# Half-rotary embedding on one core: loads and stores moved from one DMA queue to two

## The chip, the cores and the metric

The kernel runs on 1 core of one Trainium2 chip. The metric is device time in microseconds (us): 161.47 us before, median of 3 runs (161.44 to 161.71). The data lies in HBM, the main memory; the engines work on SBUF, which has 128 partitions. DMA transfers between the two are issued by the engines' sequencers, each into a queue of its own (SP's, ACT's, POOL's), and carried by 16 DMA engines.

## The reference

`x` is float32 of shape (16, 512, 16, 64): batch, sequence, heads, dim. `cos` and `sin` are (512, 32). Only the first half of the last axis is rotated; the second half is copied.

```
half = 32; x1, x2 = x[..., :32], x[..., 32:]
a, b = x1[..., :16], x1[..., 16:]
c, s = cos[..., :16], sin[..., :16]       # broadcast over batch and heads
out  = concat(a*c - b*s, a*s + b*c, x2)
```

Input and output are 33.55 MB each. There is no matrix product.

## The kernel before

**Tiles.** `x`, flat, is cut into T = 4 tiles of 8.39 MB, numbered 0 to 3. In a tile every partition holds K = 16 sequence positions of one batch element, 16 x 16 x 64 floats: 64 KB in one contiguous run in HBM. So a transfer of a whole tile has 128 runs of 64 KB; half a tile (KC = 8 positions) has 128 runs of 32 KB. SBUF holds `ring`, NS = 3 slots of one tile; tile t lies in slot t % 3, so tile 3 takes slot 0 after tile 0 has been stored.

**Tables.** `cos` and `sin` come by POOL's queue into `stage` (L63, L64). A shuffle (L73) and copies (L80, L83) on VectorE (DVE) make `table`, in which each partition has the cosines and sines of its positions.

**Compute.** `rotate(t, lo, hi)` turns half a tile in place with four DVE instructions: `b_t = x1 * s` (L96, into PSUM), `x1 = x1 * c` (L97), a subtraction (L98) and an addition (L101). Two `rotate` make a tile (`turn`), followed by one `store`. All arithmetic is on DVE, in program order: tile 0 to tile 3.

**Transfers.** `load` (L55) and `store` (L58) both issue from SP, so that all of them stand in one queue, in the order of the program. SP works its list strictly in order; an instruction that waits holds back those after it:

1. load 0, load 1, first half of load 2, with nothing to wait for
2. store 0, when tile 0 is rotated
3. second half of load 2
4. positions 0 to 13 of load 3 (KL = 14), which wait until store 0 has landed, since they overwrite its slot; then positions 14 and 15 of load 3
5. store 1, which by an explicit dependency (L115) also waits until the larger part of load 3 has landed
6. store 2 and store 3, each when its tile is rotated

The first `rotate` of a tile waits for the load that holds its half.

Of the kernel before, what the change touches and what calls it, by code (L numbers as in the profile page):

```python
# [1 line left out]

# [4 lines left out]


@with_exitstack
def kernel(  # L10
    ctx: ExitStack,
    tc: tile.TileContext,
    x: bass.AP,
    cos: bass.AP,
    sin: bass.AP,
    out: bass.AP,
):
    nc = tc.nc
    fp32 = mybir.dt.float32
    P = 128  # L20
    B, S, H, D = x.shape
    Q = D // 4
    HF = D // 2

    K = 16
    T = B * S // (P * K)
    PB = S // K
    REP = P // PB  # L30
    R = H * D
    NS = 3
    KC = K // 2
    KL = 14

    xf = x.rearrange("b s h d -> (b s h d)").rearrange("(t p f) -> t p f", t=T, p=P)
    of = out.rearrange("b s h d -> (b s h d)").rearrange("(t p f) -> t p f", t=T, p=P)
    cosf = cos.rearrange("(p k) j -> p (k j)", k=K)
    sinf = sin.rearrange("(p k) j -> p (k j)", k=K)

    const_pool = ctx.enter_context(tc.tile_pool(name="const", bufs=1))
    b_pool = ctx.enter_context(tc.tile_pool(name="bp", bufs=1, space=bass.MemoryType.PSUM))


    ring = const_pool.tile([P, NS, K, H, D], fp32)
    stage = const_pool.tile([P, 2, K, HF], fp32)
    spun = const_pool.tile([P, 2 * K, Q], fp32)
    packed = const_pool.tile([PB, 2 * K, Q], fp32)
    table = const_pool.tile([P, 2, K, 2, Q], fp32)

    def rows(t, lo, hi):
        return ring[:, t % NS, lo:hi].rearrange("p k h d -> p (k h d)")

    def load(t, lo=0, hi=K):
        return nc.sync.dma_start(out=rows(t, lo, hi), in_=xf[t, :, lo * R : hi * R])  # L55

    def store(t, lo=0, hi=K):
        return nc.sync.dma_start(out=of[t, :, lo * R : hi * R], in_=rows(t, lo, hi))  # L58


    nc.vector.memset(stage[:, :, :, 0:Q], 0.0)  # L61
    spread = stage.rearrange("(j b) t k i -> j b t (k i)", b=REP)
    nc.gpsimd.dma_start(out=spread[:, 0, 0], in_=cosf)  # L63
    nc.gpsimd.dma_start(out=spread[:, 0, 1], in_=sinf)  # L64
    load(0)
    load(1)
    load(2, 0, KC)

    PQ = PB // REP
    nc.vector.stream_shuffle(  # L73
        out=spun[:],
        in_=stage.rearrange("p t k j -> p (t k) j")[:, :, 0:Q],
        mask=[j % PQ * REP for j in range(PB)],
    )
    for q in reversed(range(REP)):
        n = PQ * (q + 1)
        nc.vector.tensor_copy(out=packed[0:n], in_=spun[q * PB : q * PB + n])  # L80

    for r in range(REP):
        nc.vector.tensor_copy(  # L83
            out=table[r * PB : (r + 1) * PB].rearrange("p t k c j -> p (t k) c j"),
            in_=packed.unsqueeze(2).to_broadcast((PB, 2 * K, 2, Q)),
        )
    C = table[:, 0].rearrange("p k c j -> p k (c j)")
    Sn = table[:, 1].rearrange("p k c j -> p k (c j)")

    def rotate(t, lo, hi):  # L90
        x1 = ring[:, t % NS, lo:hi, :, 0:HF]
        c = C[:, lo:hi].unsqueeze(2).to_broadcast((P, hi - lo, H, HF))
        s = Sn[:, lo:hi].unsqueeze(2).to_broadcast((P, hi - lo, H, HF))
        b_full = b_pool.tile([P, KC, H, HF], fp32, name="b_t")
        b_t = b_full[:, 0 : hi - lo]
        nc.vector.tensor_mul(out=b_t, in0=x1, in1=s)  # L96
        nc.vector.tensor_mul(out=x1, in0=x1, in1=c)  # L97
        nc.vector.tensor_sub(  # L98
            out=x1[:, :, :, 0:Q], in0=x1[:, :, :, 0:Q], in1=b_t[:, :, :, Q:HF]
        )  # L100
        nc.vector.tensor_add(  # L101
            out=x1[:, :, :, Q:HF], in0=x1[:, :, :, Q:HF], in1=b_t[:, :, :, 0:Q]
        )

    def turn(t):
        rotate(t, 0, KC)
        rotate(t, KC, K)
        return store(t)

    turn(0)  # L110
    load(2, KC, K)
    near = load(3, 0, KL)
    load(3, KL, K)

    tc.add_manual_dep(  # L115
        turn(1).ins,
        near.ins.name,
        mybir.DependencyInfo(mybir.DependencyClass.Sync, mybir.DependencyReason.DATA),
        reason="the store follows the loads at the DMA engines",
    )  # L120
    turn(2)
    turn(3)


# [1 line left out]
_INS = ['x', 'cos', 'sin']  # L126
_OUTS = [((16, 512, 16, 64), 'float32')]


# [23 lines left out]
```

## Time and profile before

| what | value |
|---|---|
| median of 3 runs | 161.47 us |
| the profiled execution, its own time | 162.1 us |
| its span, first to last instruction | 160.3 us |
| DVE busy | 112.4 us (70%), 43 instructions |
| packets of SP's queue, share of 16 DMA engines' span | 97.6% |
| mean DMA rate over the span | 419 GB/s |

The span is the time from the first to the last instruction of the profiled execution; some time lies around it. Engine times are sums of instructions. A DMA engine moves a transfer in packets; the share of a queue is the time that its packets took on all 16 engines. A wait is listed as the instruction that waited, an arrow, and what released it. "SPq" is SP's sequencer, which issues transfers and waits for them. "To landing" is the time from the issue of a transfer to its completion. `L58` is line 58 of the kernel.

### The profile page before, as it was taken

The numbers are of one execution on the slowest core, as the hardware profiler recorded it, in microseconds if no ns is written. First come the engines' busy times: TensorE is split into PE (matmuls) and PEld (weight loads), VectorE is DVE, ScalarE is ACT, GpSimd is POOL, SyncE is SP. The second block draws the span as 40 slices with busy tenths as digits, with TensorE's granted clock in tenths as the row PEclk, the third lists the DMA queues.
The fourth block names the chain that finished last, engine by engine and source line by source line (L and its number), as shares of the span: only waits on it lengthen the run. The fifth ranks groups of instructions, "written<-read, shape, count | busy, mean of one in ns | idle before, by whom it ended". The sixth has DMA issues, their size and how long they took to land.

```text
span 160.3 us, 113 instructions
## 1 busy us (share of the span) xinstructions
DVE 112.4 (70%) x43; POOL 1.4 (1%) x6
## 2 busy tenths in 40 slices
DVE  1000959999999999999999999999999950000000
POOL 3000000000000000000000000000000000000000
DMA  7969969699699996999999995996996996996990
GB/s 262 540 262 540 491 294 523 278 507 491 294 392 441 474 523 262 523 392 392 499 482 458 458 444 253 546 523 262 523 523 262 523 507 278 523 507 278 523 507 16
DMA packets 1504, 67.24 MB, mean 419 GB/s; under 512 B 192, under 2 KB 192, under 8 KB 224
## 3 DMA queue, kind: packets, MB, share of 16 engines
q1 hardware_dynamic: 1440, 67.11, 97.6%
q0 software_dynamic: 64, 0.13, 0.2%
HBM read 33.69 MB, written 33.55 MB: 419 GB/s over the span
## 4 chain that ended last, share of the span: by engine, by line
DVE 59%; DMA 14%; issue 7%; DVEq 1%
DVE b_t L96 22%; DVE ring L97 22%; DMA ring<-in_x_dram 14%; DVE ring L101 10%; DVE ring L98 4%; DVEq L148 1%; DVEq L96 0%
## 5 line engine op out<-in xcount | busy, mean ns | idle before, releaser
L96 DVE TENSOR_TENSOR b_t<-ring,table 128x4096 f32<-128x4096 f32 x8 | 35.5, 4432 | 2.1 <-DMA ring<-in_x_dram 1.9
L97 DVE TENSOR_TENSOR ring<-ring,table 128x4096 f32<-128x4096 f32 x8 | 35.4, 4424 | 0.3
L98 DVE TENSOR_TENSOR ring<-ring,b_t 128x2048 f32<-128x2048 f32 x8 | 18.3, 2287 | 0.3
L101 DVE TENSOR_TENSOR ring<-ring,b_t 128x2048 f32<-128x2048 f32 x8 | 18.2, 2280 | 0.0
L73 DVE LOAD_MASK_SELECT spun<-stage x1 | 0.0, 14 | 14.4 <-DMA stage<-in_sin_dram 14.4
L83 DVE COPY table<-packed 32x1024 f32<-32x1024 f32 x4 | 2.7, 684 | 0.1
L80 DVE COPY packed<-spun 32x512 f32<-32x512 f32 (+3 forms) x4 | 1.7, 416 | 0.1
L61 DVE MEMSET stage<- 128x512 f32 x1 | 0.5, 485 | 0.9 <-PEq L137 0.9
L73 DVE STREAM_SHUFFLE spun<-stage 128x512 f32<-128x512 f32 x1 | 0.7, 723 | 0.0
L63 POOL DMA_DIRECT2D stage<-in_cos_dram x1 | 0.6, 649 | 1.3 <-DVE stage L61 1.3
L64 POOL DMA_DIRECT2D stage<-in_sin_dram x1 | 0.5, 532 | 0.0
L137 POOL MEMSET const-float32-0.0<- 128x1 f32 x1 | 0.1, 93 | 0.2 <-issue 0.2
L137 POOL MEMSET const-bfloat16-1.0<- 128x1 bf16 x1 | 0.1, 95 | 0.0
L137 POOL MEMSET const-uint8-127<- 128x1 uint8 x1 | 0.1, 93 | 0.0
L137 POOL MEMSET const-float32-1.0<- 128x1 f32 x1 | 0.1, 92 | 0.0
## 6 DMA issues: line engine op xcount, KB each, us to landing
ring<-in_x_dram SPq DMA_DIRECT2D x2, 4096.0 KB, 41.4
ring<-in_x_dram SPq DMA_DIRECT2D x1, 7168.0 KB, 26.4
ring<-in_x_dram SPq DMA_DIRECT2D x1, 1024.0 KB, 28.5
stage<-in_cos_dram POOLq DMA_DIRECT2D x1, 64.0 KB, 9.0
stage<-in_sin_dram POOLq DMA_DIRECT2D x1, 64.0 KB, 13.4
out_dram<-ring SPq DMA_DIRECT2D x4, 25.6
ring<-in_x_dram SPq DMA_DIRECT2D x2, 32.0
```

The source lines that it names most:

```text
L61: nc.vector.memset(stage[:, :, :, 0:Q], 0.0)
L63: nc.gpsimd.dma_start(out=spread[:, 0, 0], in_=cosf)
L64: nc.gpsimd.dma_start(out=spread[:, 0, 1], in_=sinf)
L73: nc.vector.stream_shuffle(out=spun[:], in_=stage.rearrange("p t k j -> p (t k) j")[:, :, 0:Q], mask=[j % PQ * REP for j in range(PB)],)
L80: nc.vector.tensor_copy(out=packed[0:n], in_=spun[q * PB : q * PB + n])
L83: nc.vector.tensor_copy(out=table[r * PB : (r + 1) * PB].rearrange("p t k c j -> p (t k) c j"), in_=packed.unsqueeze(2).to_broadcast((PB, ...
L96: nc.vector.tensor_mul(out=b_t, in0=x1, in1=s)
L97: nc.vector.tensor_mul(out=x1, in0=x1, in1=c)
L98: nc.vector.tensor_sub(out=x1[:, :, :, 0:Q], in0=x1[:, :, :, 0:Q], in1=b_t[:, :, :, Q:HF])
L101: nc.vector.tensor_add(out=x1[:, :, :, Q:HF], in0=x1[:, :, :, Q:HF], in1=b_t[:, :, :, 0:Q])
L137: nc = _bacc.Bacc("TRN2", target_bir_lowering=False, num_devices=1)
L148: with _tile.TileContext(nc) as tc:
```

## The change

`load` stays on SP's queue, `store` goes to ACT's queue, which held no transfer before. Load 2 is issued whole (64 KB runs). Load 3 is issued as two halves of 8 positions (32 KB runs) in place of 14 and 2 positions. Store 1 is issued as two halves (32 KB runs), each after the `rotate` of its half. The explicit dependency of store 1 on load 3 goes. What each transfer waits for is otherwise the same: a store for the `rotate` of what it stores, load 3 for the landing of store 0.

```diff
-    KL = 14
...
     def load(t, lo=0, hi=K):
-        return nc.sync.dma_start(out=rows(t, lo, hi), in_=xf[t, :, lo * R : hi * R])
+        nc.sync.dma_start(out=rows(t, lo, hi), in_=xf[t, :, lo * R : hi * R])

     def store(t, lo=0, hi=K):
-        return nc.sync.dma_start(out=of[t, :, lo * R : hi * R], in_=rows(t, lo, hi))
+        nc.scalar.dma_start(out=of[t, :, lo * R : hi * R], in_=rows(t, lo, hi))
...
     load(0)
     load(1)
-    load(2, 0, KC)
+    load(2)
...
-    def turn(t):
+
+    rotate(0, 0, KC)
+    rotate(0, KC, K)
+    store(0)
+    load(3, 0, KC)
+    load(3, KC, K)
+    for lo, hi in ((0, KC), (KC, K)):
+        rotate(1, lo, hi)
+        store(1, lo, hi)
+    for t in range(2, T):
         rotate(t, 0, KC)
         rotate(t, KC, K)
-        return store(t)
+        store(t)
-
-    turn(0)
-    load(2, KC, K)
-    near = load(3, 0, KL)
-    load(3, KL, K)
-
-    tc.add_manual_dep(
-        turn(1).ins,
-        near.ins.name,
-        mybir.DependencyInfo(mybir.DependencyClass.Sync, mybir.DependencyReason.DATA),
-        reason="the store follows the loads at the DMA engines",
-    )
-    turn(2)
-    turn(3)
```

In the changed kernel the four lines of `rotate` are L95, L96, L97 and L100, `load` is L54 and `store` L57.

## The prediction, made before the changed kernel ran

> **What bounds the kernel now.** I read the head of the page first, then its DMA queues, then the waits of SP's queue, then short windows of the DMA view. The page:
>
> ```profile
> span 160.3 us, 113 instructions
> DVE 112.4 (70%) x43; POOL 1.4 (1%) x6
> ...
> q1 hardware_dynamic: 1440, 67.11, 97.6%
> q0 software_dynamic: 64, 0.13, 0.2%
> ...
> L96 DVE TENSOR_TENSOR b_t<-ring,table 128x4096 f32<-128x4096 f32 x8 | 35.5, 4432 | 2.1 <-DMA ring<-in_x_dram 1.9
> ```
>
> The DMA queue is the bound: its packets fill 97.6% of 16 engines' span. 10 transfers x 128 runs are 1280 packets, and the 160 left are 16 completion writes for each transfer, so one packet is one run of a partition. The packet records give 2.418 us for a 64 KB run and 1.213 us for a 32 KB run. An engine moves 67.11 MB / 16 = 64 runs of 64 KB: 64 x 2.418 = 154.8 us. It starts at 1.7 to 2.6 us and its last run ends at about 158.6, so only some 2 us of it are not bare transfer. The chain of waits names DVE for 59% of the span, but DVE ends at 130.6 us and the last store only queues from there. SP's waits show it:
>
> ```profile
> SPq L58 <- DVE ring L101: 57.7, 3, 26.9
> SPq L58 <- DMA ring<-in_x_dram: 46.5, 2, 25.6
> SPq L148 <- DMA out_dram<-ring: 28.3, 1, 28.3
> SPq L55 <- DMA out_dram<-ring: 21.7, 1, 21.7
> ```
>
> Line by line: stores wait for DVE; the store of tile 1 waits for most of load 3; after its last issue SP waits 28.3 us; and load 3 waits 21.7 us for store 0, whose ring slot it takes. All this waiting costs nothing, because the engines always have runs queued. Landings by issue time plus time to landing: load 0 at 0.74 + 22.2 = 23.0, load 1 43.0, store 0 at 49.9 + 22.5 = 72.4, the larger part of load 3 98.9, the rest 101.4, store 1 120.8, store 2 140.0, store 3 at 130.6 + 28.7 = 159.3. DVE runs without a gap from 23.05; one `rotate` takes 13.45 us (4.43 + 4.42 + 2.29 + 2.28 and the gaps; 36.50 - 23.05).
>
> One view says how two queues share an engine: the DMA view from 7 to 13 us, where the cosine and sine tables (POOL's queue) meet load 0 (SP's):
>
> ```profile
> DMA packets 96, 3.28 MB, mean 546 GB/s; under 512 B 16, under 2 KB 16, under 8 KB 48
> ...
> q1 hardware_dynamic: 48, 3.15, 120.9%
> q0 software_dynamic: 48, 0.13, 5.5%
> ```
>
> 48 packets against 48: one of each in turn, though one is 64 KB and the other 4 KB or a 4-byte completion. The records of one engine: table run at 7.298, 64 KB run of x at 7.453, and only at 9.868 the table's completion write. So a completion also waits behind the other queue's run, here 2.4 us. Round trip 9.868 - 7.298 = 2.570 against 0.159 + 2.418 = 2.577: the switch itself is free.
>
> **What the Trainium skill says.** "DMA: Bandwidth & Descriptors", section "Queues, rings and completion order": each DMA engine goes round its queues packet by packet; the 48 to 48 agrees. "Issuing engines are not separate DMA queues": SP's and ACT's DMAs run on the same 16 engines and interleave, so no bandwidth is to be won; no run here has shown ACT's queue yet. "Where 436 GB/s comes from": a ceiling of 435 GB/s; 64 KB in 2.418 us on 16 engines is 433.6, so the rate has no room. "Latency and other measured facts": copies with loads and stores on the sync and scalar queues reach 214 GB/s each way, 428 together; the trace before, one direction at a time, makes 67.11 MB in 156.5 us = 429. Mixing should be about free, by that.
>
> **The change, part by part.** Bytes, runs (1280) and completions (160) stay; DVE's 41 instructions stay in order. SP keeps 5 loads, ACT gets 5 stores of about 0.34 us issue each on an otherwise empty engine: nothing, hidden by runs already queued. Before, the explicit dependency and SP's order gave load 3 the engines alone; now order comes from turns. Walk one engine:
>
> Up to 49.94 nothing differs but that load 2 is whole. Load 1's data ends near 42.6, so load 2 has 4 of its 8 runs done at 52.3. Store 0 is issued at 49.94; an issue took 1.0 to 1.9 us to reach the engines (load 0: issued 0.74, first packets 1.74 to 2.61), so it joins at 52.3. Four runs of each alternate: 8 x 2.418, to 71.6; load 2's completion waits one run more, to 74.5. Needed at 76.83 (start of `rotate` of tile 2): cover 2.3 us, cost nothing. The four left of store 0 run to 81.3, landing 81.7, against 72.4 before. So load 3 is issued 9.4 us later; the first half of store 1, ready since 63.4, fills the engines meanwhile.
>
> Load 3 reaches the engines near 83.3, after two runs of store 1. From 83.7 32 KB runs alternate (2.43 us a pair). The first half of load 3 ends at 83.7 + 8 x 2.43 - 1.2 = 101.9 and, its completion behind a run of store 1, lands at 103.5: just at 103.72, when DVE comes to tile 3; a stall of up to 1 us here goes into the next one. Store 1 ends at about 117.7 with two 32 KB runs of load 3 left; store 2, issued at 103.7, follows it with 64 KB runs. Two short runs, one or two runs of 2.418 between them, and the completion behind such a run: the second half lands at 122.9 (one long run met) to 125.4 (two). The 16 engines have different phases and the last one counts, so I take 125.0. DVE, free at 117.17, now stalls 8 us. The last `rotate` ends at 125.0 + 0.1 + 13.45 = 138.5 instead of 130.6.
>
> Store 2's last run still ends near 139.6 (landing 140.0): the engines did the same work without a hole. Store 3 at 138.5 must reach them by then. Load 0 is the measured case of a tile put on idle engines: 22.2 us from issue to landing, some 0.3 of it the tables' runs. Hidden if issued by 159.3 - 22.0 = 137.3. At 138.5 it lands at 160.5: +1.2 us; since some engines will still be busy when it comes, I take +1.1. Both ends: issue at 136.4 costs 0, at 138.9 1.6, and a stall of the first half cannot add. The other terms: start 0, tail 0, the split of load 3 and store 1 into halves (two runs of 1.213 against one of 2.418, 16 times on an engine) 16 x 0.008 = 0.13, against 8 x 0.007 for the 2.116 and 0.309 us pieces of load 3 and 8 x 0.008 for the halves of load 2, which go: 0. Below nothing: all that is not bare transfer is 2 us, of which 0.6 is the first packet (3.2 us against 2.418) that stays, so a gain over 1 us is excluded.
>
> Sum: span 160.3 + 1.1 = 161.4; this execution took 162.1 with 1.8 around the span, 163.2 then. The median of the runs is 161.47, 0.6 under the profiled one, so 161.47 + 1.1 = 162.6.
>
> **Rivals.** *The cover holds* (not slower): only one long run comes between the last short ones, the second half lands by 123.7, store 3 is issued by 137.3 and the engines never starve: 161.5. The profile is for it in that the 9.4 us of cover (130.6 to 140.0) exceeds the stall of the best phase; against it, 16 phases must all be good. *Mixing costs*: loads and stores at once slow the runs. No hole shows at the switch from load to store at 52.07, but there is no stretch of alternation before. About 44 turns of an engine; 0.03 us each adds 1.3 us of work and makes load 3 later too: 164 to 166. *Stores take two turns for one*: store 1 would end near 110 with load 3 half done, store 2 would go before it, and load 3 end near 139: the last `rotate` 152.5, the end near 175. The 48 to 48 speaks against it. *Order kept anyway*: if SP's loads always went first, load 3 would end near 103 as before and the time stay at 161.5; this goes with the first rival.
>
> **How the numbers follow.** Store 3 late by 0.4 to 2.2 us: 0.50, 161.9 to 163.7. Cover holds: 0.25, 161.2 to 161.8. Mixing costs: 0.17, to 166. Two turns for one: 0.03. A gain of up to 1 us from something not seen: 0.05. The range 161.3 to 165.2 leaves out most of the gain, the tail of mixing and the two-for-one case. Faster by over 0.2% 0.06, within it 0.24, slower 0.70; 0.2% (0.3 us) is about what the measurement can tell.
>
> **What would show it.** Two hardware queues of 720 packets each; store 0 landing near 81.7; DVE waiting about 8 us at L95 for the last load; store 3 issued at 136 to 139; a thin slice of DMA near 140. Right mechanism and wrong phase: the wait is 6 us or less and no thin slice. Mixing shows as runs over 2.418 us, or as a larger share of 16 engines than 97.6% x 160.3 us = 156.5 us. A landing of load 3 past 128 would say that the turns are not one for one.

## The result: 165.61 us against 161.58, and the profile after

The changed kernel takes 165.61 us (median of 4 runs, lowest 165.52), the kernel before 161.58 beside it: a ratio of 1.0248, 95% interval 1.0229 to 1.0266. That is 4.0 us more, where 1.1 was forecast. One of the four executions, the one profiled first, took 168.06 us, because in two of its 16 engines load 3 met one long run more; the lines below are of a second profiled execution, 165.76 us, and are held against a second one of the kernel before, 161.53 us with a span of 159.8.

The page of the changed kernel:

```profile
span 163.6 us, 113 instructions
...
DMA  7959979988999899979899999999988996659955
...
q1 hardware_dynamic: 720, 33.55, 48.6%
q10 hardware_dynamic: 720, 33.55, 47.4%
...
L95 DVE TENSOR_TENSOR b_t<-ring,table 128x4096 f32<-128x4096 f32 x8 | 35.5, 4433 | 13.3 <-DMA ring<-in_x_dram 13.1
```

There are two hardware queues of 720 packets now: q1 is SP's, q10 ACT's. DVE sat idle for 13.3 us ahead of the first instruction of a `rotate`, against 2.1 before. The DMA digits (6, 6 and 5 from 135 to 147 us) are only a hint, since the kernel before has sixes in its row too; the windows below decide.

The timeline says when DVE waited. The columns are start, duration, engine and line, and in brackets the idle time ahead. The start of the last `rotate` in the kernel before, and then three starts in the changed kernel, the second and third of them those of tile 3:

```profile
117.17 4.43 DVE L96 TENSOR_TENSOR b_t<-ring,table 128x4096 f32<-128x4096 f32 x1
```

```profile
90.31 4.43 DVE L95 TENSOR_TENSOR b_t<-ring,table 128x4096 f32<-128x4096 f32 x1
105.38 4.43 DVE L95 TENSOR_TENSOR b_t<-ring,table 128x4096 f32<-128x4096 f32 x1 [1.66 <-DMA ring<-in_x_dram]
128.35 4.43 DVE L95 TENSOR_TENSOR b_t<-ring,table 128x4096 f32<-128x4096 f32 x1 [9.55 <-DMA ring<-in_x_dram]
```

The halves of load 3 land at 105.3 and 128.25 us, and DVE stands still for both. The last `rotate` therefore ends at 141.8 instead of 130.6. The chain of what released what shows the path to it, from store 0 through load 3 to DVE (start, duration, what):

```profile
49.97 32.33 DMA out_dram<-ring
...
82.76 45.49 DMA ring<-in_x_dram
...
128.35 4.45 DVE b_t L95
```

Meanwhile the DMA engines run dry; stretches of the DMA share (columns: stretch, length, DVE, POOL, clock, DMA share, GB/s):

```profile
120.00:139.00 19.00, 10.58 (x3) 0.00 (x0) 1.00 1.01 436
139.50:142.60 3.10, 2.26 (x2) 0.00 (x0) 1.00 0.00 0
```

Every DMA engine stands idle for 2.7 to 3.6 us, from the end of its last run of store 2 (139.2 to 140.0) until store 3 starts (142.6 to 142.8). This is the hole that the experiments below are about. By landings: store 2 lands at 140.33 against 139.45 in the kernel before, 0.88 later; store 3 (162.53 against 158.72) follows it by 22.20 us instead of 19.27, 2.93 more. That makes the 3.81 us between the spans 163.58 and 159.77. The remaining 0.4 lies around the span: 165.76 - 163.58 = 2.18 us against 161.53 - 159.77 = 1.76.

So three sums are to be explained: 2.9 us at the hole, 0.9 us ahead of it, 0.4 us around the span.

### The profile page after: what moved, and what is told of

It is laid out like the page before. It is cut to its first block, busy times and chain, and to the rows that moved or that the text cites. A ratio compares the mean times of both kernels' runs of the same rounds, so it can differ in the third digit from the quotient of the medians.

```text
span 165.9 us, 113 instructions
## 1 busy us (share of the span) xinstructions
DVE 112.3 (68%) x43; POOL 1.4 (1%) x6
## 4 chain that ended last, share of the span: by engine, by line
DMA 62%; DVE 22%; issue 2%; DVEq 1%; SPq 0%
DMA ring<-in_x_dram 42%; DMA out_dram<-ring 20%; DVE b_t L95 8%; DVE ring L96 8%; DVE ring L97 3%; DVE ring L100 3%; DVEq L142 1%; SPq L54 0%; DVEq L95 0%
## 5 line engine op out<-in xcount | busy, mean ns | idle before, releaser
L95 DVE TENSOR_TENSOR b_t<-ring,table 128x4096 f32<-128x4096 f32 x8 | 35.5, 4432 | 15.7 <-DMA ring<-in_x_dram 15.5
L96 DVE TENSOR_TENSOR ring<-ring,table 128x4096 f32<-128x4096 f32 x8 | 35.4, 4424 | 0.3
L97 DVE TENSOR_TENSOR ring<-ring,b_t 128x2048 f32<-128x2048 f32 x8 | 18.3, 2286 | 0.3
L100 DVE TENSOR_TENSOR ring<-ring,b_t 128x2048 f32<-128x2048 f32 x8 | 18.2, 2280 | 0.0
## 6 DMA issues: line engine op xcount, KB each, us to landing
stage<-in_sin_dram POOLq DMA_DIRECT2D x1, 64.0 KB, 13.3
```

Source lines behind the costliest of these rows:

```text
L97: nc.vector.tensor_sub(out=x1[:, :, :, 0:Q], in0=x1[:, :, :, 0:Q], in1=b_t[:, :, :, Q:HF])
L100: nc.vector.tensor_add(out=x1[:, :, :, Q:HF], in0=x1[:, :, :, Q:HF], in1=b_t[:, :, :, 0:Q])
```

## The experiments

### Filling the hole, and making load 3 land sooner

**Store 3 in halves.** Against the changed kernel:

```diff
-    for t in range(2, T):
-        rotate(t, 0, KC)
-        rotate(t, KC, K)
-        store(t)
+    rotate(2, 0, KC)
+    rotate(2, KC, K)
+    store(2)
+    for lo, hi in ((0, KC), (KC, K)):
+        rotate(3, lo, hi)
+        store(3, lo, hi)
```

> The changed kernel, with store 3 issued as two halves, each after its rotate. Theory (the hole): the whole loss is the time in which the engines have nothing to do before store 3, because load 3 lands late. The first half of store 3 is then ready near 120 us, stands behind store 2 and fills the engines from 139 to 149, and the second half comes near 141: time 161.4 to 162.0, no hole, DVE still waiting 8 to 11 us for the last load. Rival (mixing): alternating loads and stores slows the transfers themselves; then the time stays at 163.0 to 165.6 and the engines are busy to the end.

Measured: 163.08 us, ratio to before 1.0103 (1.0084 to 1.0122), 2.5 us under the changed kernel. Its waits, and the DMA share where the hole was:

```profile
DVE b_t L95 <- DMA ring<-in_x_dram: 15.1, 3, 11.2
```

```profile
139.50:142.60 3.10, 3.10 (x2) 0.00 (x0) 1.00 0.98 423
```

DVE waits even longer than in the changed kernel (11.2 us for the last load, against 9.55), and it costs nothing any more: the first half of store 3 covers it. The hole is the large part of the loss. But 1.6 us over the kernel before remain, more than this theory allowed.

**Store 2 in 32 KB runs**, issued at the same moment: `store(2)` becomes `store(2, 0, KC)` and `store(2, KC, K)`, both after its second `rotate`.

> The changed kernel, with store 2 issued as two halves (32 KB runs) at the same moment as before. Theory (turns against long runs): the last three runs of load 3 and its completion each stand behind a 64 KB run of store 2; with 32 KB runs the second half lands 3.5 us sooner, near 124.5 instead of 128, store 3 is issued near 138 and the time is 161.6 to 162.6. Rival (the late start alone): load 3 started too late whatever follows; landing near 127, time 164.5 to 165.6.

Measured: 162.99 us (1.0092, 1.0072 to 1.0111). The second half of load 3 lands at 125.8, DVE waits 6.0 us for it, the hole shrinks to 0.6 us. So the size of the runs in the other queue bears on when load 3 ends. The landing came 1.3 us after the expected one, and the time lies 0.4 us above the expected range; 1.6 us had been left unexplained by the first experiment.

**Store 1 in quarters:**

```diff
-        store(1, lo, hi)
+        store(1, lo, lo + KC // 2)
+        store(1, lo + KC // 2, hi)
```

> The changed kernel, with store 1 issued in four quarters (16 KB runs) at the same moments as its halves. Turns by number: load 3 (32 KB runs) gets two thirds of the engines, its second half lands near 116 and the time is 161.4 to 162.0. For the late start of load 3 (its first run began 3.6 us after the issue, behind four 32 KB runs of store 1): if an engine holds a number of runs ahead, four runs of 16 KB take 2.4 us and load 3 begins 2 to 2.6 us after its issue; if it is a time, it begins 3.4 us or more after it, behind six or seven runs. Rival (shares by bytes): the second half lands past 124, time above 164.

Measured: 162.87 us (1.0088, 1.0066 to 1.0110). With 16 KB runs against 32 KB, load 3 gets two thirds of the engines' time (from 86.5 to 103 us 161 packets of SP's queue against 163 of ACT's, and 66.7% of the time) and lands at 115.6; DVE has no wait at all for it, as its waits show (the 1.8 is load 0's):

```profile
DVE b_t L95 <- DMA ring<-in_x_dram: 1.8, 1, 1.8
```

The turns go by number of runs, not by bytes. The time is again above the expected range. For the late start of load 3, compare who runs right after its issue, at 82.4 us here and 82.3 us with quarters. Changed kernel, DMA view of 82.4 to 86.0 us:

```profile
DMA packets 48, 1.57 MB, mean 437 GB/s; under 512 B 0, under 2 KB 0, under 8 KB 0
...
q10 hardware_dynamic: 47, 1.54, 99.0%
q1 hardware_dynamic: 1, 0.03, 2.1%
```

Quarters, 81.9 to 86.2 us:

```profile
q10 hardware_dynamic: 106, 1.74, 94.1%
q1 hardware_dynamic: 8, 0.26, 14.1%
```

In the first, the 32 KB run of store 1 that is under way at the issue and three more pass on nearly every engine before the first run of load 3 (at 86.0 to 86.8 us); in the second, the 16 KB run under way and mostly six more (at 85.9 to 86.7 us). A fixed number of runs would have been the same four. It is a time, of 3.6 us or more from the issue, or an amount, of some 112 to 128 KB for each engine; these runs can't tell the two apart. Once both run, the turns are even. Changed kernel, 86.5 to 103 us (16 of the 115 are completions, which took a turn each):

```profile
q1 hardware_dynamic: 114, 3.74, 52.4%
q10 hardware_dynamic: 115, 3.24, 45.5%
```

**Store 0 alone.** A first attempt put the second half of load 2 on ACT's queue in the line after `store(0)`:

```diff
-    load(2)
+    load(2, 0, KC)
...
     store(0)
+    nc.scalar.dma_start(out=rows(2, KC, K), in_=xf[2, :, KC * R : K * R])
```

> The changed kernel, with the second half of load 2 issued on ACT's queue behind store 0, so that store 0 has the engines to itself again. Theory (store 0 late): store 0 lands near 73 instead of 82, load 3 is issued 9 us sooner and its second half lands near 117, so that DVE has no wait of more than 1 us after the first load: time 161.4 to 162.0. Rival (the sharing of load 3 and store 1 is the cause, not store 0): the last load lands past 122, time above 163.

Measured: 168.12 us. It doesn't test what it was meant to: the load, which waits for nothing, was placed at the head of ACT's list and ran beside load 0, so that DVE started nearly 10 us late. With an ordering dependency from the load to store 0:

> As l2b_behind_s0 was meant: the second half of load 2 on ACT's queue, issued after store 0 and not ahead of everything. Theory (store 0 late, because it shares the engines with load 2): store 0 lands near 73 to 74, load 3 is issued then, its second half lands near 117 and DVE loses less than 1 us: 162.5 to 163.2, the level of the runs without a hole. Rival (the sharing of load 3 and store 1 is enough): second half past 122, above 164.

Measured: 162.70 us (1.0069, 1.0054 to 1.0084). Store 0 lands at 72.7 instead of 82.3, the second half of load 3 at 116.2, and DVE waits for no load but the first:

```profile
DVE b_t L95 <- DMA ring<-in_x_dram: 1.9, 1, 1.9
```

So there are two ways to the same cure: let store 0 land in time, or give load 3 more of the turns.

### What stays without a hole: 1.1 to 1.6 us

In what follows, the loss of the engines at some place is what their runs take there beyond the usual time of their size (2.418 us for 64 KB, 1.213 us for 32 KB), as a mean over the 16 engines.

**The first use of ACT's queue.** The kernel with quarters, and the two table loads on ACT's queue in place of POOL's:

> The kernel with store 1 in quarters (162.87 us, no hole at the end), with the two small table loads on ACT's queue in place of POOL's, so that ACT's queue is used from the start. Theory (first use): the 1.2 us that every engine loses when store 0 joins, and the 0.4 us around the span, belong to the first use of ACT's queue; used early they are hidden or gone, 161.3 to 162.3. Rival (the loss belongs to the join of a store with loads under way): the same 1.2 us at store 0, time 162.6 to 163.2.

Measured: 162.70 us (1.0068, 1.0053 to 1.0083). The engines still lose 1.16 us where store 0 joins (1.09 with the tables on POOL's queue), 2.2 us still lie around the span. (The tables arrive later this way and DVE starts 3 us later, which leaves the time as it was.) First use is not it. Nor is it the meeting with load 2 alone: where the second half of load 2 was put behind store 0, store 0's own first run is long, by 0.88 us.

**One queue.** The changed kernel with `store` back on `nc.sync`:

> The changed kernel with the stores back on SP's queue, run sizes and program order as in the changed kernel (the first half of store 1 then stands ahead of load 3 in SP's list and covers the landing of store 0). Theory (the second queue costs): without turns load 3 follows the first half of store 1 in one piece and lands near 111, nothing stalls, no start of a second queue: 161.3 to 161.9, equal to the kernel before. Rival (the late, whole store 0 or the run sizes cost by themselves): 162.7 or more.

Measured: 162.99 us (1.0093, 1.0062 to 1.0125), the rival's side. Its waits:

```profile
DVE b_t L95 <- DMA ring<-in_x_dram: 1.8, 1, 1.8
```

No stall, no hole, no second queue, and still 1.4 us more than before. In the packet records every engine's last run of load 2, the one ahead of store 0, takes 3.1 to 3.8 us in place of 2.418 (a loss of 1.06 us), and 2.14 to 2.20 us lie around the span.

**The kernel before with its stores on ACT's queue**, nothing else changed:

> The kernel before with its stores on ACT's queue, nothing else changed: load 2 in halves, load 3 as 14 and 2 positions, store 1 still waiting for the larger part of load 3. Store 0 now takes turns with the second half of load 2 and lands near 82; nothing is left to run until load 3 starts, so a hole of 1 to 3 us near 82; then load 3 alone, near 104, and no stall at the end. Theory: the price of starting the second queue (1.0 us in the span and 0.4 around it, as in the runs without a hole) plus the hole: 163.8 to 166. Rival (the second queue itself is free, the price is of the alternation): 162.5 to 163.5, the hole alone.

Measured: 164.76 us (1.0195, 1.0178 to 1.0212), within the theory's range: the second queue alone costs 3.2 us, against 4.0 for the whole change, though by a hole at another place. The engines lose 1.08 us where store 0 joins; the 0.4 us around the span, which the theory had put down to the second queue too, are not there (1.73 to 1.80). Store 0 lands at 82.3 here too, and nothing is left to run until load 3 comes: the engines stand idle for 2.1 us on the mean. The DMA view from 81 to 85 us, in 40 slices of 0.1 us, shows the hole as a row of zeros:

```profile
DMA  0000000000000000000000099909990900000000
```

(A digit shows runs that start in a slice, so the zeros after the nines are runs under way; those ahead of them are idle once store 0's last run has ended, at 81.2 to 81.9.) Load 3, issued at 82.4, starts at 83.3 to 84.1: on idle engines 1.0 to 1.7 us after its issue, not the 3.6 or more of busy ones.

**The whole load 2.** All kernels so far with load 2 whole have 2.14 to 2.23 us around the span, those with halves 1.73 to 1.82. `load(2)` was made two halves in the kernel with one queue, and in the changed kernel:

> The kernel of one_queue with load 2 issued as two halves (32 KB runs), which is the last thing of the start that still differs from the kernel before. Two losses of one_queue against before are open: 1.1 us that every engine loses in the run ahead of the first store, and 0.4 us around the span (2.17 against 1.75 us in every kernel that issues load 2 whole). If both come with the whole load 2: time 161.3 to 161.8, 1.75 around the span, no long run at the first store. If only the 0.4 does: 162.3 to 162.8. If neither: 162.7 to 163.5.

Measured: 162.55 us (1.0057, 1.0038 to 1.0077), 1.73 to 1.78 around the span; the loss at the first store stays (0.86).

> The changed kernel with load 2 issued as two halves. The turns of store 0 with load 2 and the landing of store 0 near 82 stay, so load 3 is late as before and the hole before store 3 stays. Theory (0.4 us around the span belong to the whole load 2): 165.0 to 165.4, 1.75 around the span. Rival: 165.6, 2.2 around it.

Measured: 167.44 us (1.0353, 1.0332 to 1.0374), 1.77 to 1.81 around the span. The 0.4 goes with the whole load 2 in 14 kernels out of 14. The time missed its expectation: the completion of load 3's second half came at 129.6 and 129.9 us in two engines, one long run of 2.4 us later than in the other 14 (127.2 to 128.0), and the landing waits for the last engine.

**The two kernels once more**, for a second profile of each:

> The kernel before once more, for a second profile: the first one, with a span of 160.3 us against 159.7 in the timed executions, has 0.9 us of longer runs spread over loads 1 and 2 and none at the first store. If those were of that execution alone, this span is 159.4 to 159.8 and the runs are all at 2.418 us; if the first store costs something in this kernel too, a run near 52 us is long.

Span 159.77: no long runs at 52, but a loss of 0.45 us at 68 to 71, where store 0 gives way to load 2. So neither the 0.9 us of the first profile nor its place belongs to the kernel.

> The changed kernel once more, for a profile of an execution near its median: the second half of load 3 lands near 128 in all 16 engines (in the first profile 127.5 to 127.9 in 14 and 130.6 in the last), DVE waits 8 to 9 us for it, store 3 is issued near 141.5, and the span is 163.4.

Close to it: 128.25, a wait of 9.55, store 3 issued at 141.8, span 163.6.

**The place of store 0.** One queue again, store 0 between the halves of load 2:

> The kernel of one_queue_l2h (162.55 us: all on SP's queue, no stall, no hole, yet above the kernel before) with store 0 issued between the halves of load 2, as in the kernel before; load 3 and store 1 stay in halves. If the rest of the loss hangs on where store 0 stands (its first run came right after all of load 2 and made the run ahead of it 0.9 us longer): 161.3 to 161.9, no long run at the first store. If it hangs on the sizes and order of load 3 and store 1: 162.3 to 162.9.

Measured: 162.56 us (1.0064, 1.0050 to 1.0078). The long run at the first store is gone, and the time is the same: the last run of load 3 ahead of store 1, near 98.8, now takes 1.6 to 2.1 us in place of 1.213 (a loss of 0.73). The loss had moved to the next change from load to store. In both, that store had been issued long before its turn.

**The explicit dependency.** The kernel before, without it:

```diff
-    tc.add_manual_dep(turn(1).ins, near.ins.name, ...)
+    turn(1)
```

> The kernel before without its explicit dependency and nothing else: store 1 is issued when tile 1 is rotated (near 77) and stands some 24 us behind load 3 in the same queue, in place of being issued near 99 with 2 us of load 3 left. In the runs so far the run ahead of a change from load to store was 0.7 to 1.1 us long where the store had been issued well ahead (store 0 in one_queue, store 1 in s0_between), and not where it was issued 1.5 to 2 us ahead (stores 0 and 1 of the kernel before, store 0 in s0_between). Theory (a store queued early behind loads costs the engines about 1 us at the change): 162.2 to 162.8, long runs near 98 to 101. Rival (the dependency does nothing for the time): 161.4 to 161.9.

Measured: 162.62 us (1.0063, 1.0049 to 1.0077). SP's issues in the two kernels, first with the dependency and then without; the columns are start, length of the merged stretch, what, and how many:

```profile
98.41 32.54 SPq L58 DMA_DIRECT2D out_dram<-ring  x3
```

```profile
76.73 54.12 SPq L58 DMA_DIRECT2D out_dram<-ring  x3
```

Store 1 is issued 22 us sooner, and that makes the kernel 1.0 us slower: the 8 KB runs of load 3 just ahead of store 1 take up to 0.73 us against 0.309 in the kernel before, a loss of 0.80 us in the packet records. The change drops this dependency too, but with two queues this cost isn't seen: in the second profile of the changed kernel no run between 80 and 121 us is long. What the changed kernel loses, 1.18 and 1.19 us in its two profiles, it loses where store 0 joins load 2, at 51 to 55 us, and the kernel before with its stores on ACT's queue, which keeps the dependency, loses 1.08 us there. Whether the two losses have one cause is not shown.

An early issue doesn't always cost that much. In the kernel with one queue the second half of store 1 is issued at 83.3 us, 27 us before its turn behind load 3, and the engines lose 0.28 us there; with load 2 in halves 0.04 us.

Not one of these kernels beats the kernel before.

## Why the prediction was wrong

**Right: the mechanism and the side.** Store 0 shares the engines with load 2 and lands at 82.3 (81.7 predicted); load 3 is issued 10 us later (9.4 predicted); it alternates one for one; DVE waits for its second half (9.55 us, 8 predicted); store 3 comes too late and the engines run dry near 140. Load 2, whole, was in time, at 72.6. The experiments that fill the hole or let load 3 land sooner take back 2.5 to 2.9 us (the 2.9 with load 2 in two parts, which has 0.4 us less around the span).

That store 0's landing came out so near is partly luck. Load 1 landed 0.7 us sooner than in the profile that the walk used (42.3 against 43.0), and the join cost 1.2 us that the walk didn't have.

**Wrong: "Load 3 reaches the engines near 83.3, after two runs of store 1".** The 1.0 to 1.9 us behind this came from load 0, which met idle engines. Load 3 met busy ones and started at 86.0 to 86.8 us, 3.6 us or more after its issue and after four runs of store 1. (Store 0 too joined later than the walk had it, at 54.6 us or after and not at 52.3. There it mattered little, since store 0 ends after load 2 either way.) So store 1, which had the engines longer, ended at 116.2 to 117.0 us and not at 117.7, and three runs of load 3 were left and not two. The first of them followed at once; the other two, and the completion, each stood behind a 64 KB run of store 2:

```profile
DMA packets 78, 4.00 MB, mean 421 GB/s; under 512 B 1, under 2 KB 1, under 8 KB 1
...
q10 hardware_dynamic: 45, 2.95, 71.6%
q1 hardware_dynamic: 33, 1.05, 25.5%
```

(The changed kernel, 117.6 to 127.1 us: 45 runs of 64 KB against 32 of 32 KB and one completion, so two thirds of the bytes and more go to store 2.) The prediction had the landing at 122.9 if one long run is met and at 125.4 if two are; it was three. A short and a long run more are 1.21 + 2.42 = 3.6 us, less the 0.7 us by which store 1 ended sooner in the last engine: 2.9 us. The second half landed at 128.25, 2.85 us after 125.4, and store 3 was issued at 141.8 and not at 138.5.

The condition for a hole was right but too strict: store 3 on idle engines took 20.7 us to land, where 22.0 had been used. With 20.7 an issue at 138.5 would have cost next to nothing. The term of the hole, put at 1.1, measured 2.9.

One of the signs misled as well. A landing of load 3 past 128 was to say that the turns are not one for one; it came past 128 with turns that are (114 packets to 115).

**Wrong: "The other terms: start 0, tail 0".** Two terms were missing: 0.4 us around the span, which goes with issuing load 2 whole, and 0.9 us ahead of the hole, most of it where store 0 joins (1.19 us, against a loss of 0.45 us elsewhere in the second profile of the kernel before). I had called the switch between queues free on the evidence of the table loads. For runs in turn that held: the 32 KB runs from 83 to 120 us kept 1.213 us and the engines moved 430 GB/s. So the rival of mixing is out as a price of every turn; as a price paid once, at the join, there is something in it. No view of the kernel before showed a store that joins loads under way, and what the explicit dependency is worth was not asked either; in one queue it is 1.0 us.

The three terms, 2.9 + 0.9 + 0.4 = 4.2 us, are parts of the difference between the two profiled executions, so they must add up. Experiments confirm two of them: the time falls by 2.5 us when the hole is filled, and the 0.4 us go when load 2 is issued in halves. The 0.9 us are placed by the packet records, but no run with two queues took the loss at the join away, and its cause stays open.

Of the other rivals, two turns for one is refuted (114 to 115), order kept anyway too (load 3 ended at 128 and not near 103), and the cover did not hold. The prediction's 41 DVE instructions are 43 on the page; nothing hangs on it.

## What to carry to other kernels

When two queues feed busy engines, count turns by runs and not by bytes, start the count of the newcomer at a time measured on busy engines, and give the transfer that competes with the one that compute waits for the shorter runs. A completion takes its turn as well. A store that is ready early need not be issued early: in one queue, behind loads, it cost 1.0 us more here than a wait that issued it just before its turn.

## What the runs showed of the hardware that was not expected

- Load 3, joining engines busy with store 1, started 3.4 us or more after its issue in every kernel where it did so, after the run under way and, mostly, three more of 32 KB or six more of 16 KB. Store 0, taking turns with load 2 from another queue, started 4.3 us or more after its issue. On idle engines a transfer started after 1.0 to 1.9 us.
- In one queue, a store issued long before its turn behind loads made the loads' last runs longer, by 0.7 to 1.1 us on the mean of the engines, in four kernels: at store 0 with one queue and load 2 whole or in halves, at store 1 with store 0 between the halves, and at store 1 of the kernel before without its dependency. One issued 1.1 to 2.5 us before its turn did not (stores 0 and 1 of the kernel before), and the second half of store 1, behind load 3 in one queue, lost 0.28 and 0.04 us. That the early issue of store 1 costs is shown by the dependency taken out; what in the engines does it, and why it is sometimes small, stays open.
- Issuing load 2 whole goes with 0.4 us more outside the span than issuing it in parts (2.14 to 2.23 against 1.73 to 1.83 us). Why is open.
